# Attention heads of a Hymba-style encoder: k loaded once per head and doubled by GpSimd, low part of joined rows later

## Chip, cores and metric

The kernel runs on one core of one Trainium2 chip. Times are device microseconds of one whole execution. A TensorE granted clock of 1.00 in the profile is the upper of its two levels (2.4 GHz), 0.50 the lower (1.2 GHz).

## What is computed

One layer of an encoder trunk for two streams, 1024 sample rows and 256 prompt rows, 1024 wide, all in float32: a half-weighted SwiGLU block, a mixer, a second SwiGLU block, each inside RMS norms. The mixer projects a row to q, k and v of eight heads of 64 and to a gated convolution, and joins both through `w_out`. Cut to what matters here:

```python
def mixer(h, w_in, ..., w_out):
    q, k, v, ga, gb = jnp.split(h @ w_in, ...)
    attn = dilated_attention(q, k, v)            # 8 heads of 64
    ...
    return jnp.concatenate([attn, c], axis=-1) @ w_out

def dilated_attention(q, k, v):
    # three branches (window, dilation) = (128,1), (512,4), (2048,16):
    # 64 keys a side each, ALiBi bias, softmax per branch
    w = jax.nn.softmax(jnp.stack(lses), axis=0)  # merged by their denominators
    return jnp.sum(w[..., None] * jnp.stack(outs), axis=0)
```

## The kernel before, in words

Matrix products keep float32 accuracy by splitting a number into a high part of a shorter format and a low part, the remainder. Attention (`attn`, from L774) runs between the projection and `w_out`, 1199.5 to about 1350 us into the span; only it is changed.

**Operands.** q, k and v of the projection lie in DRAM (`qd`, `kd`, `vd`), q and k as high and low parts. A head's q tile has the 64 rows of q's high part in partitions 0 to 63 and its low part in 64 to 127. The two k tiles, kH and kL, hold the same 64 rows of k twice, in both halves of the partitions, so that one matmul against q of 128 partitions gives (q high + q low) x k high, and a second one adds the product with k low. `load_qk` (L795 to L803) issues this for a head on SyncE's queue: two loads for q and four for k, of 320 KB each. `cast_qb` (L805) has GpSimd write a permuted copy of q, `qb`. Tiles q, qb, k and v exist twice, for even and odd heads; head h+2 is loaded after the last use of head h.

**Steps.** A head has nine groups of scores, two units of 128 x 256 each. The loop from L1038 walks over 72 groups and places around each the older work by lag: `qk_group` (L827) does for each unit a matmul with kH (L853) and one with kL (L854) into a PSUM bank `pss`, then VectorE adds the bias and takes the minimum (L858). `exp_group` (L861) is ScalarE's exponential (L864), and after group 8 it issues `load_qk` of head h+2. Four groups later `t_group` (L937) transposes the weights on TensorE (L935) into a bank `pst`, which ScalarE (L931) or, for groups 1, 4 and 7, VectorE (L929) copies to `pT`; two groups after that `pv_group` multiplies by v (L963) into `ob`, `oa` or `op`. The banks of `pss`, `pst`, `op` and `psm` are the same four.

**End of a head.** `when(lag, 8, f)` calls f that many groups after a head's last group: `merge1` (GpSimd copies, L884), `merge2` and `merge4` (VectorE on 128x8 tiles, L892 to L907), `merge5` (a transpose, L912, and a round trip through DRAM, L917 and L924, which spreads the branch weights `x` over 64 rows). With lag 8 comes `cast_qb` of head h+2. After each odd head two heads are joined: ScalarE copies `ob` and `oa` to SBUF (L977, L1006), `combine1` (lag 10) has GpSimd multiply them by the weights (L1013, two operations), and `combine2` (lag 13) does for each half of the columns: on GpSimd hi = ta + tb, rounded to the short format (L1022), on VectorE ta = ta + tb in place (L1023) and lo = ta - hi (L1024). L1023 overwrites what L1022 reads, so it waits for it.

**Order.** The program is built with `schedule_with_timeline_sim=True` (L1313): a scheduler sets the order of the instructions of every engine from the calls and their dependences. Within an engine, that order is then fixed.

Of the kernel before, what the change touches and what calls it, by code (L numbers as in the profile page):

```python
# [10 lines left out]
F32 = mybir.dt.float32  # L11
# [17 lines left out]
NH = 8  # L29
HD = 64  # L30
# [118 lines left out]
class Trunk:  # L149
# [624 lines left out]
    def attn(self, qk, pool, rpool, qd, kd, vd, after):  # L774
        nc = self.nc
        mm = nc.tensor.matmul
        H = {}

        KW = 288
        bufs = []  # L780
        for i in range(2):
            q = qk[i].tile([P, NT], F32R, name=f"q{i}")
            qb = qk[i].tile([P, NS], F32R, name=f"qb{i}")
            k = [qk[i].tile([P, 5, KW], F32R, name=f"k{z}{i}") for z in "HL"]
# [10 lines left out]
        def load_qk(h):  # L795
            d = H.setdefault(h, {})
            q, qb, k, d["v"] = bufs[h % 2]
            f = slice(h * HD, (h + 1) * HD)
            for i in range(2):
                nc.sync.dma_start(q[i * HD:(i + 1) * HD].bitcast(F32), qd[i, f, :])  # L800
            for z, o, s in ((0, 0, 0), (0, HD, 0), (1, 0, 1), (1, HD, 1)):
                nc.sync.dma_start(k[z][o:o + HD, :, 16:16 + 256].bitcast(F32), kd[s, f, :].rearrange("f (c i) -> f c i", c=5))
            d["q"], d["qb"], d["k"] = q, qb, k  # L803

        def cast_qb(h):  # L805
            q, qb = bufs[h % 2][0:2]
            nc.gpsimd.tensor_copy(qb.rearrange("p (b c j) -> p b c j", b=8, c=4),
                                  q[:, 0:NS].rearrange("p (c b j) -> p b c j", b=8, c=4).bitcast(F32))

        def load_v(h):  # L810
            o = h % 2 * HD
            v = bufs[h % 2][3][:, :, o:o + HD]
            vh = vd[:, :, h * HD:(h + 1) * HD]
            for c in range(5):
                nc.sync.dma_start(v[:, 2 * c:2 * c + 2, :], vh[c, 16:272, :].rearrange("(b p) d -> p b d", p=P))
            for c in range(4):
                nc.sync.dma_start(v[c * 32:(c + 1) * 32, 10:19, :], vh[c].rearrange("(j i) d -> i j d", i=32))
# [9 lines left out]
        def qk_group(h, g):  # L827
            d = H[h]
            if g == 0:
                d["st"] = self.stp.tile([P, 36], F32, name="ast", tag="ast", bufs=3)  # L830
                d["P"] = {}
            ps = self.bank("pss").rearrange("p (u n) -> p u n", u=2)
            pt = rpool.tile([P, 2, 256], F32, name="pr", tag="pr", bufs=8)
            st = d["st"]
            kh, kl = d["k"]
            tabs = []
            for i in range(2):
                u = 2 * g + i
                if g < 5:
                    lh = d["q"][:, u * P:(u + 1) * P]  # L840
                    rh, rl = kh[:, g, 16:272], kl[:, g, 16:272]
                    t0 = (384 if g == 4 else 0) + P * (1 - i)
                    tabs.append(tab[0][:, t0:t0 + 256])
                    o = ps[:, i]
                else:
                    b = u - 10
                    lh = d["qb"][:, b * P:(b + 1) * P]
                    rh, rl = (bass.AP(tensor=z.tensor, offset=z.offset + 32 * b, ap=[z.ap[0], [32, 2], [KW, 4], [1, 32]])
                              for z in (kh, kl))
                    t0 = 256 if b == 0 else 512 if b == 7 else 0  # L850
                    tabs.append(tab[1][:, t0:t0 + 256])
                    o = ps[:, i].rearrange("p (s c j) -> p s c j", s=2, c=4)
                mm(o, lh, rh, start=True, stop=False)  # L853
                mm(o, lh, rl, start=False, stop=True)  # L854
                d["P"][u] = pt[:, i]
            for i in range(2):
                u = 2 * g + i
                nc.vector.tensor_tensor_reduce(out=pt[:, i], in0=ps[:, i], in1=tabs[i], scale=1.0, scalar=-NEG, op0=OP.add,  # L858
                                               op1=OP.min, accum_out=st[:, 2 * u:2 * u + 1])

        def exp_group(h, g):  # L861
            d = H[h]
            for u in (2 * g, 2 * g + 1):
                nc.scalar.activation(d["P"][u], d["P"][u], AF.Exp, bias=d["st"][:, 2 * u:2 * u + 1], scale=-1.0,  # L864
                                     accum_out=d["st"][:, 2 * u + 1:2 * u + 2])
            next_tab(h, g)
            if g == 8 and h + 2 < NH:
                load_qk(h + 2)
# [73 lines left out]
        def t_group(h, g):  # L942
            d = H[h]
            ps = self.bank("pst")
            k = GROUPS[g]
            if g < 5:
                for kb in range(2):
                    for i in range(2):
                        tr(ps, kb * 256 + i * P, d["P"][2 * g + i][:, kb * P:(kb + 1) * P])
            elif g == 6:  # L950
                tr(ps, 0, band(h, 6, 1))
                tr(ps, P, band(h, 6, 0))
                tr(ps, 256, band(h, 0, 0))
                tr(ps, 384, band(h, 8, 1))
            else:
                for i, j in enumerate(k):
                    tr(ps, i * 256, band(h, j, 1))
                    tr(ps, i * 256 + P, band(h, j, 0))
            d["T", g] = evac(g, ps)
# [55 lines left out]
        def combine2(h):  # L1015
            d = H[h]
            if h % 2:
                ta, tb = d["t"]
                for t in range(2):
                    c = slice(t * 512, (t + 1) * 512)  # L1020
                    hi, lo = (z[:, h // 2, :] for z in self.hT[t])
                    nc.gpsimd.tensor_tensor(hi, ta[:, c], tb[:, c], op=OP.add)  # L1022
                    nc.vector.tensor_tensor(ta[:, c], ta[:, c], tb[:, c], op=OP.add)  # L1023
                    nc.vector.tensor_tensor(lo, ta[:, c], hi.bitcast(F32), op=OP.subtract)  # L1024

        seq = [(h, g) for h in range(NH) for g in range(9)]
        LAG, LAG2 = 4, 2
        load_qk(0)
        load_v(0)
        load_qk(1)  # L1030
        load_v(1)
        cast_qb(0)
        cast_qb(1)

        def at(i):
            return seq[i] if 0 <= i < len(seq) else (-1, -1)

        for i in range(len(seq) + LAG + LAG2 + 11):  # L1038
            def when(k, g, f):
                h, gg = at(i - k)  # L1040
                if gg == g and h >= 0:
                    f(h)

            hq, gq = at(i)
            ht, gt = at(i - LAG)
            hv, gv = at(i - LAG - LAG2)
            if ht >= 0:
                t_group(ht, gt)
            when(5, 8, merge5)
            when(3, 8, merge3)  # L1050
            if hq >= 0:
                qk_group(hq, gq)
            when(2, 4, prompt_norm)
            when(1, 8, merge1)
            when(2, 8, merge2)
            when(4, 8, merge4)
            when(8, 8, lambda h: cast_qb(h + 2) if h + 2 < NH else None)
            when(13, 8, combine2)
            if hv >= 0:
                pv_group(hv, gv)  # L1060
                if gv == 8 and hv + 2 < NH:
                    load_v(hv + 2)
            if hq >= 0:
                exp_group(hq, gq)
                after.get((hq, gq), lambda: None)()
            when(10, 8, combine1)
# [250 lines left out]
```

## Time and profile before

| | us |
|---|---|
| median of 3 runs | 2361.45 |
| lowest and highest | 2358.35 and 2366.57 |
| profiled execution | 2363.5 |
| its span | 2361.7 |
| mean granted TensorE clock | 0.987 |

The profiled execution is one run with its own time; 1.8 us of it lie around the span. The page gives busy time per engine over the span. Windows give it for a stretch; a timeline has start, duration and, in brackets, the idle time before an instruction with what ended it; waits sum such idle times by what ended them.

### The profile page before, as it was taken

To read this page: it belongs to the slowest core of one execution; us is meant where nothing else is said; L and a number is where in the kernel's file an instruction comes from. 1 tells how busy PE (TensorE), PEld (TensorE's weight loads), DVE (VectorE), ACT (ScalarE), POOL (GpSimd) and SP (SyncE) were. 2 spreads that over 40 slices of the span, in tenths; PEclk is the share of its full clock that TensorE was granted. 3 is DMA by queue.
4 is the path that set the end of the run, shared out by engine and by line. 5 is a ranking of instruction groups with operands and counts; after the bars stand their busy time and mean duration, and the time that the engine had idled before them with its cause. 6 is when DMAs were issued, how large, how long until landed. Compare 5 with 4: busy or idle time off the path is not lost.

```text
span 2361.7 us, 30596 instructions
## 1 busy us (share of the span) xinstructions
PE 2287.1 (97%) x11788; PEld 1958.5 (83%) x11788; DVE 1277.8 (54%) x1796; ACT 809.4 (34%) x1530; POOL 674.1 (29%) x702
## 2 busy tenths in 40 slices
PE   7999999999999999999998999999999999999996
PEld 6888888888788887888887878888888888788885
DVE  5744343444454567998466833834444444545457
ACT  4322222223221234665377722322222222312123
POOL 2332232321000034897125443223233232000004
PEclk8999999999999999999999999999999999999998
DMA  4222212214332333341279642122221222423224
GB/s 158 63 64 63 79 63 70 76 59 130 96 100 79 104 111 125 96 117 49 97 162 173 159 132 98 52 79 63 70 72 63 70 76 77 156 74 94 85 80 154
DMA packets 209240, 223.51 MB, mean 95 GB/s; under 512 B 31012, under 2 KB 161060, under 8 KB 209094
## 3 DMA queue, kind: packets, MB, share of 16 engines
q1 hardware_dynamic: 209094, 221.56, 31.6%
q8 instruction: 92, 1.51, 0.3%
q14 instruction: 54, 0.44, 0.1%
HBM read 163.52 MB, written 58.00 MB: 94 GB/s over the span
## 4 chain that ended last, share of the span: by engine, by line
PE 88%; DVE 3%; DMA 3%; issue 2%; ACT 2%; POOL 2%; SPq 0%; POOLq 0%; ACTq 0%; DVEq 0%
PE psAB L198 8%; PE psAB L199 8%; PE psAB L200 8%; PE psd L198 7%; PE psd L199 7%; PE psd L200 7%; PE psR L199 3%; PE psR L200 3%; PE psR L198 3%; PE psC L198 3%; PE psC L199 3%; PE psC L200 3%; PE psgu L198 2%; PE psgu L199 2%; PE psgu L200 2%
## 5 line engine op out<-in xcount | busy, mean ns | idle before, releaser
L115 DVE TENSOR_TENSOR wb<-raw,wb 128x512 fp32r<-128x512 f32 x240 | 167.2, 698 | 218.6 <-ACT wb L114 213.9
L114 ACT ACTIVATE wb<-raw 128x512 fp32r<-128x512 f32 x240 | 150.7, 629 | 325.4 <-PE psAB L200 134.9
L207 POOL TENSOR_SCALAR st<-st 128x1 f32<-128x1 f32 x70 | 40.9, 584 | 638.0 <-ACT tmp L206 364.7
L198 PE MATMUL psd<-wd,ahl 128*128 128x512 f32 x500 | 197.6, 395 | 9.4 <-ACT y L563 3.8
L452 POOL TENSOR_TENSOR ac<-ac,tmp 128x512 f32<-128x512 f32 x40 | 67.4, 1685 | 464.0 <-DVE tmp L448 452.6
L199 PE MATMUL psd<-wd,ahl 128*128 128x512 f32 x500 | 196.0, 392 | 0.0
L200 PE MATMUL psd<-wd,ahl 128*128 128x512 f32 x500 | 195.9, 392 | 0.0
L534 ACT ACTIVATE ahl<-ar 128x512 fp32r<-128x512 f32 (+1 forms) x132 | 72.9, 556 | 351.8 <-PE psd L200 251.5
L199 PE MATMUL psR<-hT2l,wb 128*128 128x256 f32 x640 | 181.1, 283 | 0.0
L200 PE MATMUL psR<-hT2h,wb 128*128 128x256 f32 x640 | 180.9, 283 | 0.0
L198 PE MATMUL psR<-hT2h,wb 128*128 128x256 f32 x640 | 180.5, 282 | 0.0
L114 ACT ACTIVATE wb<-g 128x512 fp32r<-128x512 f32 x80 | 50.6, 632 | 224.9 <-POOL g L136 96.5
L198 PEld LDWEIGHTS psR<-hT2h,wb 128*128 128x128 f32 x640 | 122.2, 191 | 6.1
L199 PEld LDWEIGHTS psR<-hT2l,wb 128*128 128x128 f32 x640 | 122.2, 191 | 4.7
L198 PE MATMUL psAB<-hT0h,wb 128*128 128x512 f32 x320 | 125.7, 393 | 0.0
L198 PE MATMUL psC<-hT1h,wb 128*128 128x512 f32 x320 | 125.5, 392 | 0.0
L199 PE MATMUL psAB<-hT0l,wb 128*128 128x512 f32 x320 | 125.5, 392 | 0.0
L199 PE MATMUL psC<-hT1l,wb 128*128 128x512 f32 x320 | 125.4, 392 | 0.0
L200 PE MATMUL psAB<-hT0h,wb 128*128 128x512 f32 x320 | 124.5, 389 | 0.0
L200 PE MATMUL psC<-hT1h,wb 128*128 128x512 f32 x320 | 124.5, 389 | 0.0
L565 DVE TENSOR_TENSOR y<-y,psd 128x1024 f32<-128x1024 f32 x70 | 85.3, 1219 | 71.2 <-PE psd L200 71.2
L200 PEld LDWEIGHTS psR<-hT2h,wb 128*128 128x128 f32 x640 | 122.2, 191 | 1.6
(388 smaller groups left out, 6284.9 us busy)
## 6 DMA issues: line engine op xcount, KB each, us to landing
raw<-in_ffn_w_gu_dram SPq DMA_DIRECT2D x88, 512.0 KB
ad<-ac SPq DMA_DIRECT2D x88, 256.0 KB
g<-in_ffn_w_down_dram SPq DMA_DIRECT2D x44, 512.0 KB
ar<-ad SPq DMA_DIRECT2D x88, 256.0 KB
raw<-in_w_in_dram SPq DMA_DIRECT2D x20, 512.0 KB
ar<-ad SPq DMA_DIRECT2D x44, 128.0 KB
ad<-x SPq DMA_DIRECT2D x40, 128.0 KB
x2d<-y SPq DMA_DIRECT2D x10, 512.0 KB
```

The costliest lines, as they stand in the source:

```text
L114: nc.scalar.activation(out[:, 0], src, AF.Copy)
L115: nc.vector.tensor_tensor(out[:, 1], src, out[:, 0].bitcast(F32), op=OP.subtract)
L198: mm(out, lh[0], rh[0], start=first, stop=False, skip_group_check=more)
L199: mm(out, lh[0], rh[1], start=False, stop=False, skip_group_check=more)
L200: mm(out, lh[1], rh[0], start=False, stop=last, skip_group_check=more)
L207: nc.gpsimd.tensor_scalar(st[:, 0:1], st[:, 0:1], 1e-6 / (mul * mul), None, op0=OP.add)
L452: nc.gpsimd.tensor_tensor(a1, a1, q, op=OP.mult)
L534: nc.scalar.activation(hl[0], r, AF.Copy)
L565: nc.vector.tensor_tensor(y[b], y[b], o, op=OP.add)
```

## The change

`load_qk` loads k only into partitions 0 to 63 of kH and kL, two loads a head in place of four. A new `double_k` has GpSimd copy each to partitions 64 to 127 (64 x 5 x 256 elements, two copies a head). It is called for head h+2 at lag 8, ahead of `cast_qb`, and for heads 0 and 1 at the start. `combine2` keeps GpSimd's half; VectorE's two lines for each half move into `combine3`, called at lag 16, and still at 13 for the last head.

```diff
--- before.py
+++ after.py
@@ -798,9 +798,14 @@
             f = slice(h * HD, (h + 1) * HD)
             for i in range(2):
                 nc.sync.dma_start(q[i * HD:(i + 1) * HD].bitcast(F32), qd[i, f, :])
-            for z, o, s in ((0, 0, 0), (0, HD, 0), (1, 0, 1), (1, HD, 1)):
-                nc.sync.dma_start(k[z][o:o + HD, :, 16:16 + 256].bitcast(F32), kd[s, f, :].rearrange("f (c i) -> f c i", c=5))
+            for z in range(2):
+                nc.sync.dma_start(k[z][0:HD, :, 16:16 + 256].bitcast(F32), kd[z, f, :].rearrange("f (c i) -> f c i", c=5))
             d["q"], d["qb"], d["k"] = q, qb, k
+
+
+        def double_k(h):
+            for z in bufs[h % 2][2]:
+                nc.gpsimd.tensor_copy(z[HD:, :, 16:16 + 256], z[0:HD, :, 16:16 + 256].bitcast(F32))
 
         def cast_qb(h):
             q, qb = bufs[h % 2][0:2]
@@ -1020,6 +1025,13 @@
                     c = slice(t * 512, (t + 1) * 512)
                     hi, lo = (z[:, h // 2, :] for z in self.hT[t])
                     nc.gpsimd.tensor_tensor(hi, ta[:, c], tb[:, c], op=OP.add)
+
+        def combine3(h):
+            if h % 2:
+                ta, tb = H[h]["t"]
+                for t in range(2):
+                    c = slice(t * 512, (t + 1) * 512)
+                    hi, lo = (z[:, h // 2, :] for z in self.hT[t])
                     nc.vector.tensor_tensor(ta[:, c], ta[:, c], tb[:, c], op=OP.add)
                     nc.vector.tensor_tensor(lo, ta[:, c], hi.bitcast(F32), op=OP.subtract)
 
@@ -1029,7 +1041,9 @@
         load_v(0)
         load_qk(1)
         load_v(1)
+        double_k(0)
         cast_qb(0)
+        double_k(1)
         cast_qb(1)
 
         def at(i):
@@ -1040,6 +1054,13 @@
                 h, gg = at(i - k)
                 if gg == g and h >= 0:
                     f(h)
+
+
+            def late(k, k_last, f):
+                for lag, hs in ((k, range(NH - 1)), (k_last, (NH - 1,))):
+                    h, gg = at(i - lag)
+                    if gg == 8 and h in hs:
+                        f(h)
 
             hq, gq = at(i)
             ht, gt = at(i - LAG)
@@ -1054,8 +1075,9 @@
             when(1, 8, merge1)
             when(2, 8, merge2)
             when(4, 8, merge4)
-            when(8, 8, lambda h: cast_qb(h + 2) if h + 2 < NH else None)
+            when(8, 8, lambda h: (double_k(h + 2), cast_qb(h + 2)) if h + 2 < NH else None)
             when(13, 8, combine2)
+            late(16, 13, combine3)
             if hv >= 0:
                 pv_group(hv, gv)
                 if gv == 8 and hv + 2 < NH:
```

In the changed file the line numbers from L803 on are higher by 5: kH and kL matmuls are L858 and L859, the score operation L863, the exponential L869, ScalarE's evacuation L936, transposes L940, v matmuls L968, the copies of `ob` and `oa` L982 and L1011, GpSimd's products L1018, its sum L1027. `double_k` is L808, `cast_qb` L812; `combine3` is L1035 and L1036.

**TensorE, from the end of head 3 to the start of head 4.** `kH_9270`, `kL_9271` and `qb_9269` are of odd heads, `kH_9260`, `kL_9261` and `q_9258` of even ones. Before:

```order
L853 MATMUL pss<-kH_9270,qb_9269 128x256
L854 MATMUL pss<-kL_9271,qb_9269 128x256
L853 MATMUL pss<-kH_9270,qb_9269 128x256
L854 MATMUL pss<-kL_9271,qb_9269 128x256
L935 MATMUL pst<-ident,pr 128x128 x3
L853 MATMUL pss<-kH_9260,q_9258 128x256
L854 MATMUL pss<-kL_9261,q_9258 128x256
L853 MATMUL pss<-kH_9260,q_9258 128x256
L854 MATMUL pss<-kL_9261,q_9258 128x256
L935 MATMUL pst<-ident,pr 128x128 x8
```

The changed kernel at the same place; behind the rows shown come the rest of head 3's v matmuls, four transposes and two more matmuls with kH_9260, and only then the first with kL_9261:

```order
L858 MATMUL pss<-kH_9270,qb_9269 128x256
L859 MATMUL pss<-kL_9271,qb_9269 128x256
L940 MATMUL pst<-ident,pr 128x128 x6
L858 MATMUL pss<-kH_9260,q_9258 128x256
L940 MATMUL pst<-ident,pr 128x128 x4
L858 MATMUL pss<-kH_9260,q_9258 128x256
L940 MATMUL pst<-ident,pr 128x128
L968 MATMUL op<-pT,v_9272 128x256 x2
L968 MATMUL oa<-pT,v_9272 128x256
L968 MATMUL oa<-pT,v_9272 128x128 x2
L940 MATMUL pst<-ident,pr 128x128 x4
L968 MATMUL oa<-pT,v_9272 128x256
```

Where head 4's first scores followed three transposes, their second halves now follow all transposes and v matmuls of head 3.

**GpSimd, from the joining of heads 0 and 1 on, while head 3's scores are made.** Before:

```order
L884 COPY ax<-ast 32x2x2 x16
L1013 TENSOR_TENSOR to<-to,x 128x1024 x2
L825 TENSOR_SCALAR g<-g 128x768
L807 CAST qb_9259<-q_9258 128x1024
L1022 TENSOR_TENSOR hT0h<-to 128x512
L1022 TENSOR_TENSOR hT1h<-to 128x512
```

In the changed kernel, with the copies of head 4's k:

```order
L1018 TENSOR_TENSOR to<-to,x 128x1024 x2
L808 CAST kH_9260<-kH_9260 64x5x256
L812 CAST qb_9259<-q_9258 128x1024
L808 CAST kL_9261<-kL_9261 64x5x256
L889 COPY ax<-ast 32x2x2 x10
L1027 TENSOR_TENSOR hT0h<-to 128x512
L1027 TENSOR_TENSOR hT1h<-to 128x512
```

Both copies of k stand behind the products L1018, and the sums L1027 behind both copies and ten of the merge copies of head 3.

**VectorE, the same joining.** Before, the first L1023 stands between two groups of scores of head 3:

```order
L858 ISA pr,ast<-pss,g 128x256
L858 ISA ast 128x1
L1023 TENSOR_TENSOR to<-to 128x512
L858 ISA pr,ast<-pss,g 128x256
L858 ISA ast 128x1
```

In the changed kernel its place is among head 4's groups, ahead of the merge operations of head 3 (L897 on):

```order
L863 ISA pr,ast<-pss,g 128x256
L863 ISA ast 128x1
L1035 TENSOR_TENSOR to<-to 128x512 x2
L1036 TENSOR_TENSOR hT0l<-to,hT0h 128x512
L1036 TENSOR_TENSOR hT1l<-to,hT1h 128x512
L897 TENSOR_TENSOR ay<-ax,ast 128x8
L898 TENSOR_TENSOR ay<-ay,ax 128x8
```

So L1035 comes some seven groups later than L1023 did, and the four operations stand together.

## Rows read from the trace of the kernel before

**Rows 1.** The page: span, and busy time of each engine over it.

```profile
span 2361.7 us, 30596 instructions
...
PE 2287.1 (97%) x11788; PEld 1958.5 (83%) x11788; DVE 1277.8 (54%) x1796; ACT 809.4 (34%) x1530; POOL 674.1 (29%) x702
```

**Rows 2.** Windows: heads 2 to 5; stretch, length, busy by engine, clock, DMA, GB/s.

```profile
1234.60:1250.80 16.20, 16.20 (x116) 15.03 (x114) 11.82 (x54) 14.75 (x48) 6.57 (x18) 1.00 1.00 190
1250.80:1274.60 23.80, 18.68 (x114) 17.05 (x112) 13.69 (x54) 12.16 (x40) 14.95 (x22) 0.86 0.91 176
1274.60:1292.20 17.60, 17.22 (x120) 15.38 (x117) 13.00 (x58) 15.95 (x54) 5.98 (x18) 1.00 0.79 152
1292.20:1310.50 18.30, 16.33 (x112) 14.72 (x111) 16.91 (x54) 12.61 (x41) 15.10 (x22) 1.00 0.93 175
```

**Rows 3.** Timeline of VectorE in head 3: start, duration, operation, wait before it.

```profile
1257.43 0.42 DVE L858 CUSTOM_DVE_ANT_0 pr<-pss,g 128x256 f32<-128x256 f32 x1
...
1264.65 1.73 DVE L1023 TENSOR_TENSOR to<-to 128x512 f32<-128x512 f32 x1 [6.80 <-POOL hT0h L1022]
1266.31 0.41 DVE L858 CUSTOM_DVE_ANT_0 pr<-pss,g 128x256 f32<-128x256 f32 x1
```

**Rows 4.** Timeline of GpSimd over the same time.

```profile
1255.61 4.70 POOL L1013 TENSOR_TENSOR to<-to,x 128x1024 f32<-128x1024 f32 x2 [7.45 <-DMA x<-fd]
1260.27 2.14 POOL L825 TENSOR_SCALAR g<-g 128x768 f32<-128x768 f32 x1
1262.34 1.05 POOL L807 CAST qb<-q 128x1024 fp32r<-128x1024 f32 x1
1263.35 1.27 POOL L1022 TENSOR_TENSOR hT0h<-to 128x512 fp32r<-128x512 f32 x1
```

**Rows 5.** Timeline of TensorE: a wait in head 1, and the one in head 3.

```profile
1218.69 0.38 PE L854 MATMUL pss<-kL,q 128*128 128x256 f32 x1 [1.82 <-DMA kL<-kd]
...
1267.13 0.58 PE L853 MATMUL pss<-kH,qb 128*128 128x256 f32 x1 [5.12 <-DVE ast L858]
```

**Rows 6.** Window just behind that wait, columns as in rows 2.

```profile
1267.00:1274.00 7.00, 6.87 (x27) 6.13 (x28) 6.11 (x22) 4.16 (x15) 3.68 (x13) 0.61 0.73 158
```

**Rows 7.** DMA issues and queue from 1219 to 1345 us: packets, MB, share; KB each.

```profile
q1 hardware_dynamic: 27698, 20.82, 83.6%
...
kH<-kd SPq DMA_DIRECT2D x12, 320.0 KB
```

**Rows 8.** Groups by line and form, 1190 to 1400 us: busy, mean ns, idle before.

```profile
L864 ACT ACTIVATE pr<-pr,ast 128x256 f32<-128x256 f32 x144 | 71.5, 499 | 16.9 <-DVE ast L858 16.1
...
L884 POOL COPY ax<-ast 32x4 f32<-32x4 f32 x128 | 31.2, 244 | 13.7 <-ACT pr L864 8.9
L931 ACT ACTIVATE pT<-pst 128x512 f32<-128x512 f32 x48 | 28.1, 587 | 10.6 <-PE pst L935 10.4
...
L825 POOL TENSOR_SCALAR g<-g 128x768 f32<-128x768 f32 x7 | 15.0, 2141 | 7.9 <-DVE ast L858 7.9
...
L807 POOL CAST qb<-q 128x1024 fp32r<-128x1024 f32 x7 | 7.3, 1041 | 24.4 <-DMA q<-qd 21.7 <-PE psm L912 2.7
...
L977 ACT ACTIVATE to<-ob 128x1024 f32<-128x1024 f32 x2 | 2.0, 1016 | 0.6 <-PE ob L963 0.6
```

**Rows 9.** Chain of waits in an undisturbed head: start, duration, what.

```profile
1237.31 0.44 PE pst L935 x4
1237.75 0.88 PE oa L963 x6
```

**Rows 10.** Timeline of GpSimd in head 7.

```profile
1327.58 4.66 POOL L1013 TENSOR_TENSOR to<-to,x 128x1024 f32<-128x1024 f32 x2 [5.74 <-issue]
1332.21 2.13 POOL L825 TENSOR_SCALAR g<-g 128x768 f32<-128x768 f32 x1
```

**Rows 11.** Timeline of VectorE in head 7, over the same time.

```profile
1327.65 2.32 DVE L892 TENSOR_TENSOR ay<-ax,ast 128x8 f32<-128x8 f32 x1
...
1332.96 0.16 DVE L902 TENSOR_TENSOR ay<-ax,ay 128x8 f32<-128x8 f32 x1
```

## The prediction

> **What bounds the kernel now.** I first read the page [rows 1]: TensorE is busy for 2287.1 of 2361.7 us, and no other engine reaches 55%. Over the whole span only TensorE's own idle time can be won. The change touches attention alone, some 150 us of it, so I then cut that stretch into heads [rows 2]. Head 2 shows the undisturbed pace: 16.2 us, TensorE busy throughout, ScalarE for 14.75 us (91%), the DMA engines without a pause. Head 3 takes 23.8 us, 7.6 more, with TensorE busy for only 18.68 of them and the clock down to 0.86. Heads 4 and 5 take 17.6 and 18.3. The question is therefore what head 3 waits for, and whether something else, ScalarE first of all, is close enough behind to keep what is won.
>
> The chain in head 3 can be read from three engines. TensorE stops 5.12 us for VectorE's scores [rows 5]. VectorE makes a score at 1257.43 and the next at 1266.31; between them it stands 6.80 us in front of L1023, which waits for GpSimd's L1022 [rows 3]. GpSimd is late because its product L1013 waits 7.45 us for the transfer of the branch weights `x`, runs for 4.70 us, and two unrelated operations of 2.14 and 1.05 us stand between it and L1022 [rows 4]. So a joining that nobody needs for many microseconds holds the scores, because it stands ahead of them on VectorE. Right behind the stop the granted clock is 0.61 over 7 us [rows 6]: at most 7 x 0.39 = 2.7 us lost. 5.1 + 2.7 = 7.8 us, about the 7.6 us by which the head is long.
>
> **The change, part by part.** The sum is made against the profiled execution's 2363.5 us.
>
> *The joining, three steps later: -7.6 us.* L1035 now stands behind some four groups of head 4, so what it waits for must be done by then. GpSimd ends its products at 1260.3 and then makes two copies of k and one `qb` (1.3 + 1.05 + 1.3, below), until 1264. Ten merge copies of head 3 follow; they need its last exponentials, which without the stop come near 1267, and take 10 x 0.244 = 2.4 us [rows 8]. Two sums of 1.27 [rows 4] bring it to about 1272. Four groups of head 4 at 16.2 / 9 = 1.8 us end at 1267 + 7.2 = 1274. The wait should be gone, with some 2 us to spare. Bounds: -7.6 (all gone) to 0 (it returns in head 4). I take the whole, since the times above leave that slack.
>
> *Two loads of k fewer per head.* From 1219 to 1345 us the queue moves 20.82 MB at a share of 83.6%, and kH and kL stand with 12 loads of 320 KB each [rows 7]. Half of 24 x 0.328 = 7.9 MB goes, which leaves 16.9 MB and an estimated share of 0.68. On the path, the rows show only one wait for k, 1.82 us in head 1 [rows 5]. Two loads, 0.66 MB at 190 GB/s [rows 2], arrive 3.4 us sooner; two copies take 2.6 back. I take -0.8 (bounds -1.8 to +0.8, a copy that is late by its full length).
>
> *Sixteen copies on GpSimd: 0.* No row shows this operation. A cast of 1024 elements per partition takes 1.04 us [rows 8], so 1280 take 1.3; by the slowest one-input operation, 2.14 us for 768 elements [rows 8], it would be 3.6. I take 1.3, since `qb` is the same kind of operation, tensor_copy. 2.6 us a head (or 7.2) fit into GpSimd's 9.6 idle us of head 2 [rows 2]. If that cover went, the copies would delay the first kH and kL of the next head; those of head 4 are ready at 1261.6 and 1264, about 3 us before head 3 ends undisturbed.
>
> *The new order on TensorE: +5.0.* This is the term that I trust least. Between the last score of head 3 and the first complete score of head 4 stand 19 transposes and v matmuls worth ten of 256 columns; before, three transposes. Transposes take 0.44 us for four, v matmuls 0.88 for two of 256 columns [rows 9]: 19 x 0.11 + 10 x 0.44 = 6.5 us, and the first two scores on VectorE add 0.84 [rows 3]. TensorE has work all this time; the loss comes from ScalarE, which gets no new exponentials for 7.3 us. What it still has to do for head 3 is two exponentials (1.0), three evacuations (1.8) and two copies of `ob` and `oa` (2.0) [rows 8], 4.8 us. So ScalarE is short of work for 2.5 us, and at 91% it cannot catch up within a head; TensorE then waits for its weights. The same order stands at the start of head 6: 2 x 2.5 = 5.0. Bounds: 0 (ScalarE is behind by so much that its queue covers it) to 2 x 7.3 = 14.6 (it has nothing left). Heads 1 and 2 start in a milder form of it: +1.0 (0 to 2.5).
>
> *GpSimd against VectorE: +0.5.* In head 7, L892, a 128x8 operation, takes 2.32 us while L1013 runs [rows 10, 11], against 0.16 for L902 of the same size. Such pairs come at other places in the new order; bounds 0 to 4.6, two such operations, and I take a small share, since one joining's operations are moved away from scores.
>
> Sum: -7.6 - 0.8 + 0 + 5.0 + 1.0 + 0.5 = -1.9, so 2361.6 us for a profiled execution. The profiled one is 2.05 us over the median of 2361.45, so the forecast is 2359.5 us: a small gain that a measurement cannot tell from none. The bound for that is 0.3%, 7.1 us: 2354.4 to 2368.5.
>
> **The rivals.**
>
> A, faster: the order costs nothing. ScalarE's idle time in this stretch is mostly spent waiting for VectorE's scores, 16.1 us over all heads [rows 8], and the stop in head 3, 6.80 us on VectorE, is a good part of that [rows 3], so at other times it may carry a queue that covers the 2.5 us. Then -7.6 - 0.8 gives 2353.1, and if the excess of heads 4 and 5 over 16.2 us (1.4 and 2.1) came from the full DMA queue and goes too, 2349.6. I put it at 2352. Against it: ScalarE's 15.95 of 17.6 us in head 4 say that it, not the DMA, sets that head's length [rows 2].
>
> B, slower: the gap opens fully at both places. TensorE runs out of transposes, idles 5 us or more, and its clock falls as after the stop in head 3 [rows 5, 6], 2.7 us each time. With 7.3 for each gap the sum is -7.6 - 0.8 + 14.6 + 1.5 = +7.7, or 2369.2, and with both clock falls 2374.6; I put it at 2372. It decides from a loss of 7.0 us at each of the two places, clock included, that is a wait of 4.3. For it: four banks of PSUM are shared by scores and transposes, and half-made scores hold two of them during the gap. Against it: ScalarE's 4.8 us of leftover work are in the order.
>
> C, slower: the copies block VectorE. Rows show that a VectorE operation with two SBUF inputs is held by GpSimd's two-input product, L892 under L1013, but that L902 ran its 0.16 us inside the one-input L825 [rows 10, 11]. `double_k` has one input, so by the rows it holds nothing. If it did hold, an operation that meets a copy of 1.3 us would wait 0.65 on average; two a head for eight heads is 10.4 us, or 2370. The Trainium skill (SBUF — State Buffer, Who interferes with whom) speaks for this: it says that a VectorE instruction with two SBUF inputs contends with a GpSimd instruction that reads SBUF, and that the later one blocks fully, without an exception for one input. The trace agrees for L1013, and differs for L825.
>
> D, the wait only moves: L1035 stands in front of head 4's scores as L1023 did in head 3's, because `x` or the ten merge copies come later than worked out. Then the 7.6 us come back and the time is 2367, no change.
>
> **How the numbers follow.** The forecast has 0.38, D 0.05: together 0.43 for no change. A has 0.35: its gain is read from rows, and only an order argued on paper stands against it. B has 0.15, C 0.07: 0.22 for slower. The range is 2350 to 2372: it takes in most of A, all of C and D and the lower half of B, and leaves out some 0.15. Its low end is -9.4 from the median, which is the gain of A with a part of heads 4 and 5; its high end is +10.5, the gap in full with one clock fall.
>
> **What would show it.** The joining: no wait of VectorE for L1027 over 1 us in heads 3 and 4, and head 3 near 16 to 17 us with a clock of 1.00. The loads: share of the DMA queue near 0.68 and no wait of TensorE for k. The copies: 16 of L808 near 1.3 us; 3 us or more, and kH or kL waiting for them, would make it wrong. The order: at the starts of heads 4 and 6 ScalarE idle for 2 to 3 us ahead of its first exponential, and TensorE waiting about as long some microseconds later; no such idle time is A, 4 us and a window of 0.6 to 0.8 in the clock is B. VectorE operations on two inputs that take over 1 us while L808 runs would be C. I am wrong if attention is over 8 us shorter, or longer at all.

## The result and the profile after

The changed kernel takes 2377.4 us (median of 6, 2373.15 to 2379.71) against 2361.23: a ratio of 1.0065, 95% interval 1.0051 to 1.0080. It is slower by 16.2 us, outside the predicted range of 2350 to 2372. The profiled execution is the fastest of the six, 2373.15 us, so the trace shows less of the loss than the medians: its span is 9.7 us longer than that of the kernel before.

The page, and the GpSimd copies and the DMA queue over the stretches of rows 8 and 7:

```profile
span 2371.4 us, 30650 instructions
...
PE 2289.4 (97%) x11788; PEld 1955.9 (82%) x11788; DVE 1279.3 (54%) x1796; ACT 809.1 (34%) x1530; POOL 694.2 (29%) x718
```

```profile
L808 POOL CAST kH<-kH 64x1280 fp32r<-64x1280 f32 x7 | 8.8, 1255 | 6.1 <-DMA kH<-kd 6.0
```

```profile
q1 hardware_dynamic: 22168, 15.73, 61.5%
```

GpSimd is busier by 20.1 us, 16 copies of 1.25 us, as estimated, and no other engine by more than 2.3; the queue's share fell from 83.6% [rows 7] to 61.5%. The windows of heads 2 to 6 answer to [rows 2]:

```profile
1231.50:1250.70 19.20, 17.43 (x121) 15.86 (x118) 12.62 (x56) 14.98 (x47) 8.55 (x20) 1.00 0.74 142
1250.70:1271.70 21.00, 18.00 (x116) 16.09 (x114) 15.49 (x56) 13.60 (x46) 16.14 (x22) 0.92 0.65 127
1271.70:1295.40 23.70, 19.30 (x117) 16.54 (x114) 14.99 (x62) 14.96 (x48) 10.45 (x22) 0.93 0.57 109
1295.40:1316.00 20.60, 17.98 (x114) 16.09 (x113) 14.91 (x49) 13.53 (x46) 16.12 (x22) 0.92 0.57 115
1316.00:1339.70 23.70, 19.30 (x115) 16.55 (x114) 15.04 (x62) 14.85 (x48) 10.41 (x22) 0.93 0.48 100
```

Head 3 is 2.8 us shorter, but heads 4 and 6 take 23.7 us (before 17.6 and 17.1), heads 2 and 5 some 3 and 2 more. From the first score of head 0 to the last of head 7 attention takes 158.5 us, before 148.7; head 0 is 1.8 us longer, heads 1 and 7 are 3.3 and 4.0 shorter. TensorE's waits in attention have new names:

```profile
PE ob L968 <- ACT pT L936: 9.0, 5, 2.5
PE psm L917 <- DVE ay L912: 6.3, 4, 2.2
```

**The start of head 4.** TensorE's timeline, then ScalarE's (start, duration, operation, wait before it):

```profile
1271.68 0.37 PE L858 MATMUL pss<-kH,q 128*128 128x256 f32 x1
...
1279.16 0.47 PE L859 MATMUL pss<-kL,q 128*128 128x256 f32 x1
...
1283.56 1.13 PE L968 MATMUL ob<-pT,v 128*128 128x256 f32 x4 [1.41 <-ACT pT L936]
1286.90 0.37 PE L917 MATMUL psm<-ident,ay 128*16 128x128 f32 x1 [2.21 <-DVE ay L912]
```

```profile
1272.56 0.50 ACT L869 ACTIVATE pr<-pr,ast 128x256 f32<-128x256 f32 x1
...
1273.06 1.12 ACT L936 ACTIVATE pT<-pst 128x512 f32<-128x512 f32 x2
1274.86 0.38 ACT L989 ACTIVATE hT2h<-op 64x256 fp32r<-64x256 f32 x1 [0.69 <-PE op L968]
1277.62 0.60 ACT L936 ACTIVATE pT<-pst 128x512 f32<-128x512 f32 x1 [2.38 <-PE pst L940]
1279.55 1.03 ACT L1011 ACTIVATE tmp<-oa 128x1024 f32<-128x1024 f32 x1 [1.34 <-PE oa L968]
1280.47 0.50 ACT L869 ACTIVATE pr<-pr,ast 128x256 f32<-128x256 f32 x1
```

The first kL stands 7.5 us behind the first kH. From the end of head 3's last exponential (1273.06) to the start of head 4's first (1280.47) ScalarE has none to do for 7.4 us, and it is idle for 4.4 of them. TensorE then waits 1.41 us for weights, and 2.21 us for the merge weights of head 3, which it transposes before the next scores. Behind that its clock is at the lower level (windows, columns as in rows 2):

```profile
1283.00:1290.00 7.00, 4.23 (x19) 3.80 (x20) 5.13 (x19) 3.56 (x14) 2.62 (x7) 0.76 0.12 22
1286.50:1290.00 3.50, 3.10 (x15) 3.13 (x16) 2.04 (x8) 1.36 (x5) 0.00 (x0) 0.51 0.14 21
```

The copies were not late:

```profile
1259.12 1.28 POOL L808 CAST kH<-kH 64x1280 fp32r<-64x1280 f32 x1
1260.46 1.04 POOL L812 CAST qb<-q 128x1024 fp32r<-128x1024 f32 x1
1261.56 1.25 POOL L808 CAST kL<-kL 64x1280 fp32r<-64x1280 f32 x1
```

kL was there at 1262.8, 16 us before it was used. Here only the order made TensorE use it late.

**VectorE's merges in head 3**, under those very copies:

```profile
1259.20 1.22 DVE L899 TENSOR_TENSOR ay<-ay,ast 128x8 f32<-128x8 f32 x1
1260.70 0.82 DVE L907 TENSOR_TENSOR ay<-ax,ay 128x8 f32<-128x8 f32 x1 [0.28 <-ACT ay L902]
1261.44 0.15 DVE L908 TENSOR_TENSOR ay<-ast,ay 128x8 f32<-128x8 f32 x1
1261.63 1.20 DVE L909 TENSOR_TENSOR ay<-ay 128x8 f32<-128x8 f32 x1
```

L908, between two of them, takes 0.15 us. L899, L907 and L909 end at 1260.42, 1261.52 and 1262.83, each 0.02 us behind a copy (1260.40, 1261.50, 1262.81). So GpSimd's one-input copies hold VectorE's two-input operations, `qb`'s too.

In head 3 this hold is on the path. ScalarE waits 1.74 us for L899, of which 1.07 are the copy's (1.22 against 0.15 for L908); behind that wait, in ScalarE's fixed order, stands the evacuation L936, for which TensorE waits 1.92 us, and then 1.08 us for the merge weights of head 2, which come behind L907 and L909 (ScalarE, then TensorE):

```profile
1260.45 0.21 ACT L902 ACTIVATE ay<-ay 128x16 f32<-128x16 f32 x1 [1.74 <-DVE ay L899]
1260.58 0.58 ACT L936 ACTIVATE pT<-pst 128x512 f32<-128x512 f32 x1
```

```profile
1261.21 1.13 PE L968 MATMUL ob<-pT,v 128*128 128x256 f32 x4 [1.92 <-ACT pT L936]
1263.42 0.38 PE L917 MATMUL psm<-ident,ay 128*16 128x128 f32 x1 [1.08 <-DVE ay L912]
```

So head 3 takes 21.0 us at a clock of 0.92, though its old stop is gone.

The joining stands where the order had put it, four groups into head 4 and thus nine groups (not seven) behind its old place, without the 6.80 us [rows 3]:

```profile
1282.66 1.29 DVE L1035 TENSOR_TENSOR to<-to 128x512 f32<-128x512 f32 x2
```

### The profile page after: what moved, and what is told of

It is laid out like the page before. It is cut to its first block, busy times and chain, and to the rows that moved or that the text cites. A ratio compares the mean times of both kernels' runs of the same rounds, so it can differ in the third digit from the quotient of the medians.

```text
span 2371.4 us, 30650 instructions
## 1 busy us (share of the span) xinstructions
PE 2289.4 (97%) x11788; PEld 1955.9 (82%) x11788; DVE 1279.3 (54%) x1796; ACT 809.1 (34%) x1530; POOL 694.2 (29%) x718
## 4 chain that ended last, share of the span: by engine, by line
PE 88%; DVE 4%; ACT 3%; DMA 2%; issue 2%; POOL 2%; SPq 0%; POOLq 0%; ACTq 0%; DVEq 0%
PE psAB L198 8%; PE psAB L199 8%; PE psAB L200 8%; PE psd L198 7%; PE psd L199 7%; PE psd L200 7%; PE psR L199 3%; PE psR L200 3%; PE psR L198 3%; PE psC L198 3%; PE psC L199 3%; PE psC L200 3%; PE psgu L199 2%; PE psgu L198 2%; PE psgu L200 2%
## 5 line engine op out<-in xcount | busy, mean ns | idle before, releaser
L198 PE MATMUL psd<-wd,ahl 128*128 128x512 f32 x500 | 198.4, 397 | 10.3 <-ACT y L563 3.4
L198 PEld LDWEIGHTS psd<-wd,ahl 128*128 128x128 f32 x500 | 94.9, 190 | 34.8 <-ACT y L563 4.2
```

What stands on the lines that cost most here:

```text
L198: mm(out, lh[0], rh[0], start=first, stop=False, skip_group_check=more)
```

## The experiments

Comparisons are with runs of the kernel before in the same job (medians 2361.7 to 2363.3).

| run | loads of k | copies on | set by hand | us | ratio to before, 95% |
|---|---|---|---|---|---|
| e1_join | 4 | none | nothing; combine3 at 16 | 2362.2 | 0.9988 to 1.0012 |
| e3_order | 2 | GpSimd | TensorE's rule | 2367.1 | 1.0012 to 1.0033 |
| e4_rule | 4 | none | TensorE's rule | 2364.2 | 1.0003 to 1.0022 |
| e6_force | 4 | none | joining late | 2353.4 | 0.9952 to 0.9978 |
| e8_psm | 2 | GpSimd | rule, L917 at lag 7 | 2364.5 | 1.0001 to 1.0020 |
| e10_psm9 | 2 | GpSimd | rule, L917 at lag 9 | 2361.6 | 0.9987 to 1.0013 |
| e13_nocopy | 4 | none | rule, L917 at lag 9 | 2362.2 | 0.9988 to 1.0013 |
| e14_hold | 4 | GpSimd, constant | rule, L917 at lag 9 | 2354.7 | 0.9964 to 0.9986 |
| e16_late | 4 | none | rule, lag 9, joining late | 2352.3 | 0.9942 to 0.9972 |
| e15_drain | 4 | none | heads 4, 6 start late | 2376.5 | 1.0044 to 1.0079 |
| e5_spare_rule | 4 | GpSimd, spare | TensorE's rule | 2385.2 | 1.0083 to 1.0120 |
| e7_spare | 4 | GpSimd, spare | nothing | 2382.2 | 1.0067 to 1.0105 |
| e9_dve | 2 | VectorE | joining late | 2387.8 | 1.0086 to 1.0124 |
| e11_dve | 2 | VectorE | joining, copies late | 2367.7 | 1.0017 to 1.0042 |
| e12_ts | 2 | GpSimd, times 1.0 | rule, lag 7 | 2387.6 | 1.0096 to 1.0142 |

**The joining alone.** The change without `double_k` and with four loads.

> The joining alone: combine3 at lag 16, all else as before (four loads of k, no copies). In this program every engine's instructions stand in the same order as before. By the order theory (the loss of the change comes from the new order of TensorE's work, which double_k brought with it) and by the lock theory (it comes from GpSimd's copies of k, which hold VectorE's operations with two SBUF inputs) the time is that of before, 2361 us within 3. By the prediction's first term it would be 2354.

2362.2 us, no change. The second part of the change moves no instruction: in the trace every engine's order in attention is that of before, so the three steps of lag had no say in it. That the scheduler goes by when it believes operands ready would explain this, and is not shown. L1035 moved in the changed kernel because of `double_k`: in e7_spare (below), with four loads and copies that nobody reads, it stands in the same place.

**TensorE's order by hand.** An edge for the scheduler, which sets an order and waits for nothing:

```diff
+        def behind(ins, lead):
+            n = len(last_k) - 2 * lead - 1
...
+                self.tc.add_manual_dep(ins.ins, last_k[n].ins.name, mybir.DependencyInfo(
+                    mybir.DependencyClass.NoSync, mybir.DependencyReason.DATA), reason="order")
-                mm(o, lh, rl, start=False, stop=True)
+                last_k.append(mm(o, lh, rl, start=False, stop=True))
-            nc.tensor.transpose(ps[:, c0:c0 + P], x, self.ident)
+            behind(nc.tensor.transpose(ps[:, c0:c0 + P], x, self.ident), 0)
-            mm(out, d["v"][:, blk, :], T[:, c0:c0 + n], start=bool(first), stop=bool(last))
+            behind(mm(out, d["v"][:, blk, :], T[:, c0:c0 + n], start=bool(first), stop=bool(last)), 1)
```

> The change, with one rule for TensorE's order added: transposes of a step are issued behind the last kL matmul of the step before, and v matmuls behind that of one step earlier. Loads and copies are those of the change. Order theory: the 16 us come back, and with the fewer loads up to 5 more: 2356 to 2363 us. Lock theory: the copies still run, so at least half of the loss stays: 2369 us or more.

> The kernel before with the same rule for TensorE's order: what the rule alone does. Order theory: complete scores first is what before has too, so 2361 us within 4. Lock theory: nothing in it changes what GpSimd does, 2361 within 4. Over 2368 would say that the rule itself costs, and would have to be taken off the run with the change.

With the change 2367.1 us: 10.3 of the 16.2 are gone, though copies and loads are the same; heads 4 and 6 take 19.8 and 21.0 us. On the kernel before the rule costs some 2.4. In this run, as in e4_rule and e6_force, the scheduler also set the other engines' orders anew, so the 10.3 are the rule's with what followed from it. The largest wait of TensorE that is left with the change, in e3_order:

```profile
PE psm L923 <- DVE ay L918: 12.8, 5, 4.8
```

**The transpose of the merge weights later** (merge5 at lag 7, then 9, behind the scores of the step before).

> The change with the rule for TensorE's order (2367.1 us), and the transpose of the merge weights two steps later, behind the scores of the step before it. TensorE waited 12.8 us in five places for those weights. Lock theory, by which the copies cost only through this wait: 2356 to 2362 us. If TensorE's wait moves to the next thing instead: 2365 to 2368.

> The change with the rule for TensorE's order, and the transpose of the merge weights at lag 9 (it was 2364.5 us at lag 7, where TensorE still waited 3.6 and 3.7 us for the weights in heads 5 and 6, and its clock fell behind each). If this wait is the way in which the copies still cost: 2353 to 2359 us. If TensorE's wait moves to something else: 2363 us or more.

2364.5 and 2361.6 us: each gives back some 3, and neither all that was expected. One such step is hardly clear of noise (the intervals of neighbours overlap), the two together are. At lag 9 heads 2 to 4 take 16.3 to 16.8 us; head 5 takes 23.0, and VectorE is held there by two products of GpSimd (the first two operations, 0.68 and 0.95 us unheld) and by two copies behind them (L885, 0.61 unheld):

```profile
1289.72 2.25 DVE L1042 TENSOR_TENSOR hT1l<-to,hT1h 128x512 fp32r<-128x512 f32 x1
...
1292.49 2.51 DVE L834 SCALAR_TENSOR_TENSOR g<-g,half 128x768 f32<-128x768 f32 x1
...
1295.67 1.84 DVE L885 TENSOR_SCALAR pr<-pr,ast 128x256 f32<-128x256 f32 x2
```

**The joining really moved.** In `combine3`, on the kernel before:

```diff
-                    nc.vector.tensor_tensor(ta[:, c], ta[:, c], tb[:, c], op=OP.add)
+                    late_s(nc.vector.tensor_tensor(ta[:, c], ta[:, c], tb[:, c], op=OP.add), h)
```

where `late_s` is such an edge to the last score operation traced.

> The kernel before with the joining really moved: VectorE's ta = ta + tb is issued behind the last score operation traced at lag 16. Loads as before, no copies. If the wait of VectorE for GpSimd in head 3 (6.80 us) was on the path, as the prediction took it, 7.6 us go: 2354 us. If the wait only moves, into head 4's scores or into the operations behind it, 2359 to 2362 us.

2353.4 us, 8.4 less than before. But that is not the price of the stop in head 3 alone. Head 3 is 5.4 us shorter, now 18.4 us at a clock of 1.00; from first to last score head 7 is 5.3 us shorter (15.3, before 20.6) and head 5 1.4. Head 7 had no such stop: there two products of GpSimd held VectorE's merges [rows 10, 11], and TensorE waited behind them (VectorE, then TensorE, in the kernel before):

```profile
1330.01 2.26 DVE L893 TENSOR_TENSOR ay<-ay,ax 128x8 f32<-128x8 f32 x1
```

```profile
1333.13 1.33 PE L963 MATMUL op<-pT,v 128*128 128x256 f32 x4 [3.79 <-ACT pT L931]
```

In e6_force the same products hold one merge operation (2.37 us) in place of two, and TensorE has no wait over 0.5 us in that head.

**TensorE's order without copies or late k.** Six empty steps ahead of heads 4 and 6:

```diff
+            seq += [(-1, -1)] * (6 if h in (4, 6) else 0) + [(h, g) for g in range(9)]
```

and the first matmul of those heads behind all that is traced on TensorE.

> The kernel before (four loads, no copies) with TensorE's order of the change made by hand at two places: the first scores of heads 4 and 6 are issued behind all transposes and v matmuls of the head before, then four groups of scores follow one another. By the prediction's term (ScalarE is short of work for 2.5 us at each place) 5 us: 2366 us. By the reading of the changed trace (heads 4 and 6 took 23.7 us in place of 16.2) about 7.5 us each: 2374 to 2380 us. If the order alone is harmless and copies or late k made it cost: 2359 to 2364 us.

2376.5 us, 13.6 more than before: an order of this kind costs without copies, late k or fewer loads. But it is not 6.8 at each place. From the first scores of head 3 to those of head 5 it is 44.5 us (before 41.4), from head 5 to head 7 40.2 (before 35.4): 3.2 and 4.8. The other 5.3 us lie in head 7, where VectorE stands 5.8 us in front of GpSimd's merge copies. Nor are the 4.8 us lost at the start of head 6, where TensorE has no wait; they lie in head 5, where VectorE stands in front of GpSimd's sum at a new place (VectorE, then TensorE):

```profile
1298.03 1.73 DVE L1025 TENSOR_TENSOR tmp<-tmp 128x512 f32<-128x512 f32 x1 [3.40 <-POOL hT0h L1024]
```

```profile
1301.19 1.09 PE L937 MATMUL pst<-ident,pr 128*128 128x128 f32 x4 [3.46 <-DVE ast L860]
```

The empty steps moved joining and merges too, so this run does not price the missing exponentials alone.

**Copies on which nothing waits.** First into a spare tile, from k:

> The run with the rule on the kernel before (2364.2 us), plus 16 GpSimd copies of k (64 x 1152 elements) into a spare tile that nothing reads; four loads of k as before, so no score depends on a copy. Lock theory (the copies hold VectorE's merges, and TensorE waits for the merge weights): 2367 to 2371 us, as much as the change with the rule (2367.1). If what is left there is that copied k comes late, or that fewer loads cost, 2364 within 1.5.

> The same copies into a spare tile and four loads, without the rule. The scheduler again puts TensorE's first scores of heads 5, 6 and 7 behind transposes and v matmuls of the head before, in halves, though no data can be late. Order theory: the loss of the change is there, 2372 to 2380 us. If the order is harmless by itself and only late k cost in the changed kernel: as the run with the rule, 2364 to 2371.

2385.2 and 2382.2 us. As a price of the copies both are inconclusive: loads of k came late, and TensorE waited for them, 7.3 us in e7_spare and in e5_spare_rule:

```profile
PE pss L866 <- DMA kL<-kd: 11.6, 3, 9.8
```

The copies read tiles that the next loads overwrite; how much of the delay comes from that is not shown. One head of e7_spare says more. Head 6 starts in the very order of head 4 in the changed kernel, waits for no load, and ScalarE is idle in it for 0.69, 2.37 and 1.34 us, as there. TensorE:

```profile
1318.99 0.37 PE L859 MATMUL pss<-kH,q 128*128 128x256 f32 x1
...
1326.69 0.38 PE L860 MATMUL pss<-kL,q 128*128 128x256 f32 x1
...
1331.42 0.92 PE L969 MATMUL ob<-pT,v 128*128 128x256 f32 x3 [1.52 <-ACT pT L937]
```

The head takes 22.6 us (before 17.1), 1.8 of them a wait in front of head 7. So copies bring this order about with four loads and no reader of what they write, and the order costs where no k is late.

Then from a constant table, which no load overwrites, with each copy kept in the program's order behind `cast_qb`, beside runs without copies under the same rules:

> The run with the rule and the transpose of the merge weights at lag 9 (2361.6 us), with four loads of k and no copies: the same hand-set order without double_k. If the copies cost on GpSimd and by holding VectorE (its operations with two SBUF inputs, and in head 5 of that run one of 2.51 us and one of 2.25 us under GpSimd's work): 2350 to 2357 us, and the difference is their price. If fewer loads pay for the copies: 2361 us or more.

> As the run without copies (four loads, the rule, the transpose at lag 9), plus three GpSimd copies a head of a constant table (64 x 768) into a spare tile: nobody reads the result, and no load and no score waits for them. So they can cost only by GpSimd's time and by holding VectorE. Lock theory: 4 to 10 us over the run without copies, with VectorE's merges that end within 0.1 us of the end of a copy. If copies cost only through the order and through late k: within 2 us of the run without copies.

> Four loads, no copies, the rule for TensorE's order, the transpose of the merge weights at lag 9 (2362.2 us), and the joining really moved, behind the last score traced at lag 20. In the run at 2362.2 VectorE stood 4.7 us in front of GpSimd's sum in head 4; in the run with copies of a constant (2354.7) the joining came later of itself. If that wait explains their difference: 2350 to 2356 us, at or below the run with the copies. If the copies of a constant helped in some other way: 2360 or more.

2362.2, 2354.7 and 2352.3 us. The run with copies was faster than the first without, against both theories. In e14_hold the scheduler had put the joining later, without a wait; in e13_nocopy VectorE still stood in front of GpSimd's sum, 4.7, 1.4 and 2.8 us in three heads. The first, in e13_nocopy:

```profile
DVE to L1041 <- POOL hT0h L1033: 4.7, 1, 4.7
```

With the joining moved by hand and no copies it is 2352.3 us, the fastest of all. The 18 copies of 0.98 us thus cost little: 2.4 us by the times (2354.7 - 2352.3, from two jobs), 4.3 by the ratios, whose intervals overlap, and the joinings do not stand at the same places in the two. Yet the copies hold VectorE in e14_hold, as here L906 to 1289.14 under a copy that ends at 1289.13 (GpSimd's timeline, then VectorE's):

```profile
1288.31 0.82 POOL L816 CAST spare<-half 64x768 bf16<-64x768 f32 x1
```

```profile
1288.37 0.77 DVE L906 TENSOR_TENSOR ay<-ay,ax 128x8 f32<-128x8 f32 x1
```

**Other ways to double k.**

> The change with the rule and the transpose at lag 7 (2364.5 us), where GpSimd doubles k by a multiplication with 1.0 in place of a copy. Before, VectorE's 128x8 operations ran through this form of operation (tensor_scalar, 2.14 us for 768 elements) unheld. By that, each of the 16 takes some 3.6 us, none of VectorE's merges under it takes over 0.3 us, TensorE's waits for the merge weights are shorter, and the time is 2357 to 2363 us if holding is what costs; 2364 or more if GpSimd's time itself does (37 us more on it) or if this form holds too.

2387.6 us: this form holds too, and for longer. GpSimd, and VectorE beside it:

```profile
1334.29 3.85 POOL L814 TENSOR_SCALAR kL<-kL 64x1280 fp32r<-64x1280 f32 x1
```

```profile
1334.14 4.08 DVE L1041 TENSOR_TENSOR tmp<-tmp 128x512 f32<-128x512 f32 x2
```

Two operations of 0.69 us each take 4.08.

> Two loads of k a head, the second halves copied by VectorE (one-input copies) in place of GpSimd, and the joining really moved as in the run that gave 2353.4 us. No GpSimd copy can hold VectorE, and first scores stand complete. Order and lock theories: what is left is VectorE's own time for 16 copies, some 0.7 us each, beside a DMA queue with less in it: 2350 to 2357 us. If VectorE is the next bound (15 to 17 us busy of 17 to 18 in the heads after 3): 2360 or more.

2387.8 us. Not VectorE's busy time did most of this, as the second reading had it (a copy took 1.15 us on average, where 0.7 was estimated): VectorE stood in front of loads that had not landed:

```profile
DVE kH L815 <- DMA kH<-kd: 20.1, 6, 5.0
```

> VectorE copies k, as in the run that took 2387.8 us, but each pair of copies is issued behind the last score operation traced at lag 7, so that VectorE doesn't stand in front of a load that has not landed (20.1 us in six places there). If that wait was the loss: 2350 to 2358 us. If VectorE's own time for 16 copies (16.1 us) is on the path: 2362 or more.

2367.7 us: 20 come back, but the time stays above that of the kernel before. That VectorE's time for the copies (0.95 us each) does this is not shown. TensorE's longest wait, in head 3, stands behind merges that GpSimd's products and `qb` hold (VectorE, then TensorE):

```profile
1251.71 2.04 DVE L906 TENSOR_TENSOR ay<-ax,ast 128x8 f32<-128x8 f32 x1
1253.79 2.26 DVE L907 TENSOR_TENSOR ay<-ay,ax 128x8 f32<-128x8 f32 x1
```

```profile
1257.81 1.65 PE L977 MATMUL op<-pT,v 128*128 128x256 f32 x3 [4.73 <-ACT pT L945]
```

## Why the prediction was wrong

**Two steps failed: the order on TensorE, sized at +5.0 (+1.0 for heads 1 and 2), and the copies, put at 0 with +0.5 for holding.**

**The order.** The prediction named the mechanism and two of the places: half-made scores, no exponentials for 7.3 us (measured 7.4), TensorE waiting some microseconds later. It sized the loss by ScalarE's idle time, 2.5 us at each place. That idle time was 4.4 us, because the leftover work was not waiting in a queue but came as TensorE let it (waits of 0.69, 2.38 and 1.34 us between the pieces); and behind it TensorE waited for weights (1.41 us) and for merge weights (2.21), and its clock fell to 0.51 (3.5 x 0.49, at most 1.7 us). The rule gives back 10.3 us where the terms had 6.0: inside their own bounds, but not their size. e15_drain shows 3.2 us up to the start of head 5, near the 2.5, for an order with complete scores; its other losses have stops of VectorE of their own. Heads 4 and 6 lost 7.5 us each against 16.2, and 6.1 and 6.6 against what they took before. By the signs that the prediction gave for rival B (ScalarE idle for 4 us, a clock of 0.6 to 0.8) it came about: 4.4 us and 0.76. By its mechanism it did not: the gap did not open fully (4.4 of 7.3 us), and TensorE did not idle 5 us for lack of transposes.

**The joining, -7.6, was wrong in cause, and its size was met by luck.** The prediction took it that L1035 stands later because it is called at lag 16. e1_join shows that the call moves nothing; e6_force gives 8.4 us for a real move, but only 5.4 in head 3, whose stop was priced, and most of the rest in head 7. In the changed kernel the stop did go, as a by-product of the copies, yet head 3 is only 2.8 us shorter: other waits took its place.

**The copies, 0, and the holding, +0.5.** The duration was right (1.25 us against 1.3), and GpSimd had room. But I had ruled out rival C by L902, which ran 0.16 us inside L825 [rows 10, 11]. It began 0.75 us after L825. Elsewhere in the kernel before, GpSimd, then VectorE:

```profile
1234.29 2.14 POOL L825 TENSOR_SCALAR g<-g 128x768 f32<-128x768 f32 x1 [4.54 <-DVE ast L858]
```

```profile
1234.65 0.48 DVE L892 TENSOR_TENSOR ay<-ax,ast 128x8 f32<-128x8 f32 x1
```

L892 is held until 1235.13, 0.84 us behind L825's start; the rest of that record holds nothing, and L902 fell nearly wholly into the rest. By the rule of the Trainium skill (SBUF — State Buffer, Who interferes with whom) a VectorE instruction with two SBUF inputs contends with a GpSimd instruction that reads SBUF, and there is no exception for one input. The changed trace agrees: held operations end 0.02 us behind a copy. Rival C's mechanism and its sign (VectorE operations over 1 us under L808) were real, but its price of 10 us is not shown: a held merge costs what waits for it. In head 3 of the changed kernel ScalarE and TensorE waited for it; with the merge weights wanted late, copies of a constant cost some 2 to 4 us, hardly clear of noise; where TensorE asked for the weights at once it waited 12.8 us in e3_order, of which the holding is a part that no run here separates from the scheduler's placing of the merges.

How much the copies cost beside TensorE's order stays open. If pieces added up, -8.4 for the joining and +10.3 for the order would leave some 14 of the 16.2 us to them, where the prediction had 0, +0.5 and -0.8; that they add up is not shown.

**The loads, -0.8.** The queue's share fell to 61.5% (0.68 said; the same stretch of time holds 15.7 MB and not 16.9, since the heads are longer), and TensorE no longer waits for k. No gain can be told apart: e10_psm9 with two loads and copies and e13_nocopy with four and none agree within 1 us, each with long heads for reasons of its own.

**What brings the time back.** 10.3 us go with the rule, 2.6 with merge5 at lag 7 and 2.9 at lag 9, which is 15.8 of 16.2, with copies and two loads in place. These are what the cures give, not shares of the loss. Against e16_late, without copies and with its joining late too, e10_psm9 is still 9.3 us longer; in the traces head 5 is 5.6 us of that (23.0 against 17.4, with VectorE held), and the rest is not settled.

One figure of the forecast is wrong, and nothing rests on it: the low end of the range, 2350, is 11.4 us under the median of before, not 9.4.

## What to carry to other kernels

Where a scheduler sets the order, an edit to when a function is called may move nothing, and a new instruction may move everything else: compare the order of every engine for each part of a change alone. Give a late-used result an explicit place on the engine that waits for it; such edges on three joinings took this kernel from 2362 to 2353 us with no change to the work. Before an engine is called held or not held by another, look at several meetings of the two and at the end times, not at one duration.

## What the runs showed that was not expected

Under a GpSimd copy of one input, VectorE's two-input 128x8 operations end 0.02 us past the copy's end. L885, with one tensor input, is held as well: 1.84 us for two under two copies in e10_psm9, 0.61 unheld. For tensor_scalar on GpSimd the hold is shorter than the record: held 128x8 operations end 1.3 us before the end of a record of 2.14 (768 elements), 0.43 us before that of one of 3.4 (1280, in e12_ts).
